# Attention query tiles: two whole ScalarE copies out of PSUM, and casts, low parts and sample parts made from the copy

## The chip, the cores and the metric

The kernel runs on one core of one Trainium2 chip. The metric is device time in microseconds (us). All times of the kernel before are from three runs and one profiled execution.

## The reference, cut to what matters

One layer of a hybrid decoder is computed for 512 prompt tokens, 16 meta tokens and 32 sample tokens (8 sequences of 4): a SwiGLU feed-forward block, then a gated linear attention branch and a stick-breaking attention branch side by side, a gated output projection, and a second SwiGLU block. The change lies in the stick-breaking branch, in the projection `q_b` and in what is made of it:

```python
q_b = q_b.reshape(B, L, SB_HEADS, SB_HEAD_DIM)      # 16 heads of 64
z = jnp.einsum('bqhd,bkhd->bhqk', qblk, k).astype(jnp.float32) * scale + bias_f   # scale = 64 ** -0.5 = 0.125
l = jnp.where(mask, jax.nn.log_sigmoid(-z), 0.0)
r = lax.cumsum(l, axis=3, reverse=True) - l
a = jnp.where(mask, jnp.exp(jax.nn.log_sigmoid(z) + r), 0.0)
return jnp.einsum('bhqk,bkhd->bqhd', a.astype(v.dtype), v)
```

## The kernel before

**Precision.** A product of two fp32 matrices is made of three TensorE products in the type fp32r: each operand is written as a high part (a cast, mostly on ScalarE) plus a low part (operand minus high part, on VectorE), and high x high, high x low and low x high are summed in PSUM. So each weight tile costs a ScalarE cast and a VectorE subtraction before TensorE can use it. In the profile these are the lines L1006 (cast, in `parted`) and L172 (the helper `tt`, called by `parted_lo`) for the weights of the key and value products, and L706 for those of the queries.

**Order.** The program is one loop of steps. A generator yields after about six matmuls (`tile_steps`: eight steps for a tile; `seven_steps`: fourteen); after each yield, `step()` runs the callbacks that `later(n, f)` placed n steps ahead, and then the callbacks that a table `at` holds for that step. ScalarE, VectorE, TensorE and GpSimd work in the order in which the program issues to them, so a callback's place in that order is its place in the queue of its engine.

**The attention stage.** The 16 heads go in 8 pairs. `BEGIN[pr]` is the step at which pair `pr` begins; from pair 1 on, a pair has 8 steps for `Pair.queries` and 14 for `Pair.values_keys`, which makes keys and values together by seven products of half size (a Strassen-like form) in four PSUM accumulators a, d, b, c. Its order is: a (2 steps), d (2), b (2), d again (2), c (2), a again (2), c again (2). Between them ScalarE copies a into b (L1069, 2 steps in; b goes on from there), d into a tile `e5` (L1059, 4 steps in; TensorE's second d product has to wait for that copy), b into c (L1069, 6 steps in) and b into a tile `u2` (L1059, 6 steps in). The third of the four weight tiles, `b2`, is the one that the second d product uses: its high part is cast 2 steps in (L1006) and its low part made 3 steps in (L172).

During the same steps the scores of the pair before are worked off: `scores` (two products, then two sigmoids on ScalarE, L2010 and L2011), `scan` (L2024, VectorE), `weigh` (L172 with 1343 columns, VectorE, and two small copies, L2035), `rows_k` (four transposes, L2041, and a ScalarE copy, L2043), `turned` (transposes of the weighed scores, L2086, and ScalarE copies, L2089), `summed` (L2102). For pairs 4 to 7 ScalarE also copies turned cache keys (L2191).

**Accumulator banks.** There are four, handed out in turn. The two that `queries` fills for its halves of 280 and 264 columns are the third and fourth that `values_keys` takes right behind it: the first half's bank becomes b, the second half's bank becomes c. So the copy of a into b can't start before everything that reads the first query half has read it.

**The queries now.** When the last product of `queries` is issued, the program issues at once: four ScalarE activations (L1925; 64 partitions x 280 or 232 columns: scale by 0.125, high part into `qs`), four small VectorE instructions (L1936; the sample tokens' queries into the tiles `qz`), and four VectorE instructions (L175; the low part, from PSUM and the high part). All twelve read the two PSUM banks.

**Memory.** All work tiles but a few live in one arena, and a table `PLACES`, one byte for each `take`, says at which slot each tile of the program lies. A tile that reuses a slot waits for the last reader of the tile before.

Of the kernel before, what the change touches and what calls it, by code (L numbers as in the profile page):

```python
# [19 lines left out]
NP = 512  # L20
NS = 32
NM = 16
NT = NP + NS + NM
HW = NT // 2
# [26 lines left out]


PLACES = bytes.fromhex("""
06241813202a5c3c5478117282764a7c688e328660846e8c92747a4c7034644e58567e38486a0c04948800401e804290666c8a4452304e500d44
2e5a3a6202360c100f16125c3e20223c2a1e401464344c0c48387e70568800046a94666c06504e464290304480288a262418081c62026e8e363a
327a86605a2e7c76922a5e078310848c694a885674520c504e0d689272082e1907062c1c8d5c2a8284855a1a6950740d83680f188c56082c850a
5e4e0b5a2a0684822e520c0d74696857585083075e0b562c5c5a820d8c0c2e69842a8306587557742c0a560d5e5c690c842e680d08828d83742c
8c565c060c07845e680d826975748c0856585957065c0d0c608468748c82908670667a446c948e0f4c808a0d266e7e30486a365458281a1c4024
3e52184e501e3c5a0f8a060d272b2d2a403e245a56262c0d408a3e3f2c0e8b3c243d0d3c8a2c400d413d3f3e3c5a361e30348b3c0a061a74821c
14948a0b3f7e62428c68902b28252429404e4a58546c5634888009723e263c0b0d8e18437c3063757f698395646a12702b16460850918d451d15  # L60
1b762d2a2f2e4d1000065384020f6e923304660d0a8a0e7a76518672484c503e3c32520f3031330d0e8f8e305070326a7c52085c645e0d602236
3880203a6216685a1e4e9042467e8f44741a941d2c824a121c2e262a8d648c28245c18658e0c5e0d1458360f4c2a6a3a16541a2e628015947c75
20448e2c82306450702652658d8c22386c48297432568f5e4458420c20365c0f1c1480942890300e7c467568182c094c82086465701e22297e60
5b5030565458325a2423908e4e12888c6c340c5e25186882493a4c0e16626a7c7d4446752e787438284208604011224a524870887e6c648c142a
2c5e12341c806a68829475627c16371e5b5249250e10701e36485d5e1a121888162514280c2a78493770885b1e27522c2e123718193628162578
3b141a70522a48125b0c1e2136254a4c880c11203b52141a7810121e185d708816252a521a5b364878100c133b122118162e142a1e2c20381052
3688701e5b2512211a0d362c4c4a2c25200c783b88702e212a52181614291e122c387888365b0d3a1a1e25123870480f3617200d0c1a78522c2a
182e2188113a141a0f4c4a12255b1678881e3614100c783b12141352705c2e2a18365e1a5b2c263828780e3a521e13885e25481a702c1a521416
1270884d7836383a2e5c2a4818124a78200c0e1e2636282c561e482a545b2e5e2594341c908e4c227438102c941a141652563a365d26784a1850
2c941c201e125174565b3490248e4c5b481e2226285d1a74501814123416514a564c52788e525074942c1c1856204a1a1e5c4c2250485e561c20  # L70
541e12342e4c2b2214165b1a182d2e5212502a1f5a344e32485856541c1e22305a2e122d34522c504e2a32481614585412202248181e1c1a582c
2e248e345474350e287826884e0c7090955250943637781012343214163b74905494702e78372a2c745c4a907556393b3655324c74944a377890
363b555a06303e646200600246726604806e40763c6a428c84686c513682927e867c588e28484f4a544c8a377d7a1e0c20223a440e181c4e8988
7b241a7c263a5051122a70106a167a5456888a483637902e421478647a828e92284d4b593e587437367e6c868c7a68844e774b3c403d6e6f417a
6651796571756b11364e94153f91430004506072620238462c4c0c9476204a181c0e241e487c681a8a445a08286684888e92828c7e6c86565a7a
323034122e1614422a103c5e6a6e0b4f40643a0809382374781f2426575854285990705c3d7a273f524e2307643940223a5a24547a362141285e
25501f372738225c09540a08642639407b3c2458076551287a20081e065326563b3c3938641f365452207a501e65245853082607063b3e3c5236
2051656424223a087a533b1f063e1e365150272664243a215320381e060a7a087e64024a72346c606862368a923a26200e82428c88128e761810
942c1c2a52864e505a2e40561a362c2454182a583c1f1c1d2c191b181c592a5657581d1856581c1d591b19181a3c425a36133a14221a5718121e
1517561c067e20688886  # L80
""")


class Arena:
# [13 lines left out]
    def take(self, width, dt=F32):  # L98
        k, s = -(-width // self.UNIT), next(self.places)
        c, n = self.column(s)  # L100
        assert all(self.free[s : s + k]) and s + k <= c + n, f"no room for {width} at {s}"
        if c not in self.tile or self.tile[c].dtype != dt:
            assert all(self.free[c : c + n]), f"two types at {c}"
            self.made += 1
            self.tile[c] = self.pool.tile([P, n * self.UNIT], dt, tag=f"room{c}", name=f"room{c}_{self.made}")
        self.free[s : s + k] = [False] * k
        a = self.tile[c][:, (s - c) * self.UNIT : (s - c) * self.UNIT + width]
        self.held[id(a)] = (a, s, k)
        return a
# [27 lines left out]
def hybrid_step(  # L137
# [26 lines left out]
    def ps(tag="ps"):  # L164
        count[0] += 1
        if tag == "acc":
            banks.append(banks.pop(0))
            return pa.tile([P, 512], F32, tag=f"acc{banks[-1]}", name=f"acc{count[0]}")
        return pp.tile([P, 512], F32, tag=tag, name=f"{tag}{count[0]}")

    def tt(out, a, b, op, eng=None):
        (eng or V).tensor_tensor(out=out, in0=a, in1=b, op=op)  # L172

    def stt(out, a, s, b, op0, op1):
        V.scalar_tensor_tensor(out=out, in0=a, scalar=s, in1=b, op0=op0, op1=op1)  # L175
# [91 lines left out]
    W2 = (HW, W1)  # L267
# [25 lines left out]
    for g in range(4):  # L293
        r_ = slice(NS * g, NS * g + NS)
# [470 lines left out]
    def later(n, f):  # L765
        todo.append([n, f])
# [154 lines left out]
    class Gain:  # L921
# [586 lines left out]
    for kind, what, n in MIXER:  # L1508
        w, c = {"r": (win, C_RA), "a": (win, C_GA), "b": (win, C_GB), "o": (w_o_gla[0], 0), "p": (w_o_sb[0], 0)}[what]
# [5 lines left out]
    with tc.manual_schedule(engines={E.PE, E.DVE, E.Activation, E.Pool}):  # L1515
# [72 lines left out]
        for j in range(2):  # L1588
            c = slice(P * j, P * j + P)
# [188 lines left out]
        for e in range(2):  # L1778
            acc = {h: ps("acc") for h in range(2)}
# [13 lines left out]
        p = ps()  # L1793
        for j in range(5):
            n = P if j < 4 else NTL
# [31 lines left out]
        for hd, head in enumerate(HEADS):  # L1827
# [54 lines left out]
    def qzp(pr, more=128):  # L1882
        return qz[pr // 2][:, 256 * (pr % 2) : 256 * (pr % 2) + 128 + more]

    own_, other = (slice(0, 64), slice(64, P)), (slice(64, P), slice(0, 64))
# [17 lines left out]
    class Pair:  # L1903
# [9 lines left out]
        def queries(self):  # L1913
            pr = self.pr
            acc = yield from tile_steps(um, W1)

            self.qs = qs = [take(NP, F32R) for _ in range(2)]
            def out(part):
                for h in range(2):
                    for e in range(2):  # L1920
                        c = slice(h * HW, min(NP, h * HW + HW))
                        src = acc[h][own_[e], : c.stop - c.start]
                        hi = qs[e][own_[e], c]
                        if part == 0:
                            S.activation(hi, src, AF.Copy, scale=0.125)  # L1925
                        else:
                            stt(qs[e][other[e], c], src, 0.125, hi.bitcast(F32), ALU.mult, ALU.subtract)

            out(0)
            for e in range(2):  # L1930
                r_ = slice(64 * e, 64 * e + 64)
                for g in range(2):

                    o = qzp(pr, 160)[r_, 128 * g : 128 * g + 160].rearrange("p (b x) -> p b x", x=40)[:, :, 4 * e : 4 * e + 4]
                    src = acc[1][r_, NP - HW + 16 * g : NP - HW + 16 * g + 16].rearrange("p (b t) -> p b t", t=4)
                    V.tensor_scalar(out=o, in0=src, scalar1=0.125, scalar2=None, op0=ALU.mult)  # L1936
            out(1)

        def keys(self):
            pr = self.pr  # L1940
# [554 lines left out]
    with tc.manual_schedule(engines={E.PE, E.DVE, E.Activation, E.Pool}):  # L2495
# [8 lines left out]
        starts, n = {}, -MIX0  # L2504
# [49 lines left out]
        for pr in range(8):  # L2554
            now, n, after = Pair(pr), BEGIN[pr + 1], BEGIN[pr + 2] if pr < 7 else BEGIN[8] + 20
# [25 lines left out]
        n, w0 = BEGIN[8], Weights(0)  # L2581
# [16 lines left out]
        n = 0  # L2598
# [29 lines left out]
        n = 8 * len(PAGES)  # L2628
# [43 lines left out]
        n = 0  # L2672
# [18 lines left out]
        for i, (n, h) in enumerate([(n, 0) for n in range(8)] + [(n, 1) for n in range(7, -1, -1)]):  # L2691
# [12 lines left out]
            acc = product(ms, (h,), held[n])  # L2704
# [94 lines left out]
```

## Time and profile before

| | |
|---|---|
| median of 3 runs | 1504.53 us (1504.02 to 1506.23) |
| profiled execution, own time | 1504.86 us |
| its span, first to last instruction | 1503.2 us |
| TensorE matmul busy | 1484.8 us |
| VectorE busy | 1099.9 us |
| ScalarE busy | 821.2 us |
| mean granted TensorE clock | 0.997 |

The own time of the profiled execution lies 1.7 us over its span and 0.3 us over the median. The span's first part is the first feed-forward block, then come the projections and the gated linear attention, then the attention stage with the eight pairs (about 566 to 800 us from the span's start, pairs 1 to 7 from about 583 us on), then the gates, the output projection and the second block.

### The profile page before, as it was taken

The page shows a single profiled execution, that of the slowest core. Times are in us where ns is not written, and L with a number is a line of the kernel's source. Part 1 is how long each engine was busy: PE and PEld are TensorE (multiplying, and loading weights), DVE is VectorE, ACT ScalarE, POOL GpSimd, SP SyncE. Part 2 cuts the span into 40 slices and gives each one's busy share as a digit, 9 for nine tenths or more (in the row PEclk, how much of TensorE's full clock was granted, in tenths as well). Part 3 has the DMA queues.
Part 4 walks back from the last instruction along what each step waited for, and adds up shares of the span by engine and source line. Part 5 has one row for each costly group of instructions (what it writes and reads, how often), then busy time and mean ns, then how long its engine had stood idle before and what let it go on. Part 6 is the DMA issues. An engine that isn't in the chain of part 4 may idle for free.

```text
span 1503.2 us, 29783 instructions
## 1 busy us (share of the span) xinstructions
PE 1484.8 (99%) x11825; PEld 1431.1 (95%) x11825; DVE 1099.9 (73%) x1860; ACT 821.2 (55%) x1537; POOL 78.0 (5%) x175
## 2 busy tenths in 40 slices
PE   9999999999999999999999999999999999999998
PEld 8999999999999889888889899999999999999998
DVE  5888888954677867877777844666567898888544
ACT  6455454533655657676776643644564555455334
POOL 2000000000000011211211000000000000000000
PEclk9999999999999999999999999999999999999999
DMA  8133333324665687457577767434532333333243
GB/s 250 51 91 99 99 99 93 93 78 139 168 142 132 160 160 154 110 107 134 137 112 177 224 166 206 100 99 136 163 108 69 90 108 99 99 99 89 88 146 121
DMA packets 288541, 187.61 MB, mean 125 GB/s; under 512 B 10988, under 2 KB 266674, under 8 KB 288402
## 3 DMA queue, kind: packets, MB, share of 16 engines
q1 hardware_dynamic: 280706, 181.97, 45.7%
q0 software_dynamic: 7680, 3.74, 2.3%
q8 instruction: 93, 1.52, 0.4%
q14 instruction: 46, 0.38, 0.1%
q10 hardware_dynamic: 16, 0.00, 0.0%
HBM read 160.63 MB, written 25.03 MB: 124 GB/s over the span
## 4 chain that ended last, share of the span: by engine, by line
PE 90%; DVE 5%; ACT 3%; issue 1%; DMA 0%; DVEq 0%; ACTq 0%; SPq 0%
PE acc L1301 8%; PE acc L1302 8%; PE acc L1300 8%; PE acc L741 6%; PE acc L744 6%; PE acc L742 6%; PE acc L728 5%; PE acc L729 4%; PE acc L731 4%; PE acc L1079 3%; PE acc L1081 3%; PE acc L1080 3%; PE acc L1239 2%; PE acc L1242 2%; PE acc L1240 2%; DVE room L172 2%
## 5 line engine op out<-in xcount | busy, mean ns | idle before, releaser
L172 DVE TENSOR_TENSOR room<-room,room 128x544 fp32r<-128x544 f32 (+18 forms) x443 | 286.1, 665 | 83.6 <-ACT room L1059 18.6
L172 DVE TENSOR_TENSOR lo<-raw,hi 128x1024 fp32r<-128x1024 f32 (+1 forms) x207 | 247.9, 1198 | 100.9 <-ACT hi L1006 59.9
L1301 PE MATMUL acc<-room,hi 128*128 128x280 f32 (+1 forms) x896 | 259.9, 290 | 0.0
L1302 PE MATMUL acc<-room,lo 128*128 128x280 f32 (+1 forms) x896 | 259.4, 289 | 0.0
L1300 PE MATMUL acc<-room,hi 128*128 128x280 f32 (+1 forms) x896 | 259.2, 289 | 0.0
L1006 ACT CAST hi<-raw 128x1024 fp32r<-128x1024 f32 x114 | 119.4, 1051 | 141.8 <-PE acc L1301 48.9
L728 PE MATMUL acc<-room,hi 128*128 128x280 f32 x608 | 175.7, 306 | 0.2 <-DVE room L175 0.2
L1302 PEld LDWEIGHTS acc<-room,lo 128*128 128x128 f32 x896 | 168.9, 188 | 0.0
L1301 PEld LDWEIGHTS acc<-room,hi 128*128 128x128 f32 x896 | 168.6, 188 | 0.0
L1300 PEld LDWEIGHTS acc<-room,hi 128*128 128x128 f32 x896 | 168.6, 188 | 0.0
L729 PE MATMUL acc<-room,hi 128*128 128x280 f32 x608 | 163.7, 289 | 0.0
L1079 PE MATMUL acc<-room,hi 128*128 128x280 f32 x476 | 147.6, 310 | 2.6 <-ACT room L1059 1.8
L1081 PE MATMUL acc<-room,lo 128*128 128x280 f32 (+1 forms) x476 | 139.9, 294 | 3.4 <-DVE lo L172 3.3
L1080 PE MATMUL acc<-room,hi 128*128 128x280 f32 (+1 forms) x476 | 139.2, 293 | 0.0
L706 ACT CAST hi<-raw 128x1024 fp32r<-128x1024 f32 (+1 forms) x93 | 93.5, 1006 | 77.9 <-issue 20.4
L1006 ACT CAST hi<-room 128x1024 fp32r<-128x1024 f32 x106 | 88.9, 838 | 82.2 <-PE acc L1301 60.0
L172 DVE TENSOR_TENSOR lo<-room,hi 128x1024 fp32r<-128x1024 f32 x106 | 101.1, 953 | 43.7 <-ACT hi L1006 43.3
L731 PE MATMUL acc<-room,lo 128*128 128x280 f32 x608 | 126.0, 288 | 0.0
L728 PEld LDWEIGHTS acc<-room,hi 128*128 128x128 f32 x608 | 114.5, 188 | 7.3 <-issue 5.6
L729 PEld LDWEIGHTS acc<-room,hi 128*128 128x128 f32 x608 | 114.7, 189 | 0.6
L741 PE MATMUL acc<-room,hi 128*128 128x280 f32 (+2 forms) x388 | 110.7, 295 | 0.0
L742 PE MATMUL acc<-room,hi 128*128 128x280 f32 (+2 forms) x388 | 108.7, 290 | 0.0
(405 smaller groups left out, 3614.4 us busy)
## 6 DMA issues: line engine op xcount, KB each, us to landing
raw<-in_w_in_dram SPq DMA_DIRECT2D x68, 256.0 KB, 5.1
raw<-in_ffn_w_gate_dram SPq DMA_DIRECT2D x64, 256.0 KB, 3.1
raw<-in_ffn_w_up_dram SPq DMA_DIRECT2D x64, 256.0 KB, 3.4
raw<-in_ffn_w_down_dram SPq DMA_DIRECT2D x36, 448.0 KB, 3.8
raw<-in_w_in_dram SPq DMA_DIRECT2D x29, 512.0 KB, 7.7
out_dram<-room SPq DMA_DIRECT2D x36, 256.0 KB, 4.8
room<-in_cache_k_dram SPq DMA_DIRECT2D x32, 256.0 KB, 5.4
room<-in_cache_v_dram SPq DMA_DIRECT2D x32, 256.0 KB, 6.1
```

What stands on the lines that cost most here:

```text
L172: (eng or V).tensor_tensor(out=out, in0=a, in1=b, op=op)
L728: T.matmul(acc[h][:, :w], hi[k], act.get(k, h, w)[0], start=(k == order[0]), stop=False, skip_group_check=True)
L729: T.matmul(acc[h][:, : wid[h]], hi[k], a[h][1], start=False, stop=False, skip_group_check=True)
L731: T.matmul(acc[h][:, : wid[h]], lo[k], a[h][0], start=False, stop=(k == order[-1]), skip_group_check=True)
L741: T.matmul(acc[h][:nw, : wid[h]], wh, a[h][0], start=(k == 0), stop=False)
L742: T.matmul(acc[h][:nw, : wid[h]], wh, a[h][1], start=False, stop=False)
L1006: S.copy(hi[:, :kt], src)
L1079: T.matmul(x[:, :n], hi, act_[k][0][:, :n], start=(first and k == 0), stop=False, skip_group_check=True)
L1081: T.matmul(x[:, :w], lo, act_[k][0][:, :w], start=False, stop=(k == 3), skip_group_check=True)
L1300: T.matmul(x[:, :QW], hi, act[k][0], start=(first and k == 0), stop=False, skip_group_check=True)
L1301: T.matmul(x[:, :QW], hi, act[k][1], start=False, stop=False, skip_group_check=True)
L1302: T.matmul(x[:, :QW], lo, act[k][0], start=False, stop=(k == 3), skip_group_check=True)
```

## The change

In `Pair.queries`, two ScalarE copies move the whole accumulators (128 partitions x 280 and x 264 columns), scaled by 0.125, into one fp32 tile `qf`. Nothing else reads the PSUM banks. From `qf` the rest is made some steps later: the sample parts (four small VectorE copies) 3 steps on, the high parts (two ScalarE casts of 64 partitions x 512 columns) 6 and 9 steps on, the low parts (two VectorE subtractions of that size) 8 and 11 steps on. The tiles `qs` are taken 6 steps later than before; `qf` is held for 11 steps. As the list of tiles is another one, the table `PLACES` is another one from its first byte to its last.

```diff
-            self.qs = qs = [take(NP, F32R) for _ in range(2)]
-            def out(part):
-                for h in range(2):
-                    for e in range(2):
-                        c = slice(h * HW, min(NP, h * HW + HW))
-                        src = acc[h][own_[e], : c.stop - c.start]
-                        hi = qs[e][own_[e], c]
-                        if part == 0:
-                            S.activation(hi, src, AF.Copy, scale=0.125)
-                        else:
-                            stt(qs[e][other[e], c], src, 0.125, hi.bitcast(F32), ALU.mult, ALU.subtract)
-
-            out(0)
-            for e in range(2):
-                r_ = slice(64 * e, 64 * e + 64)
-                for g in range(2):
-
-                    o = qzp(pr, 160)[r_, 128 * g : 128 * g + 160].rearrange("p (b x) -> p b x", x=40)[:, :, 4 * e : 4 * e + 4]
-                    src = acc[1][r_, NP - HW + 16 * g : NP - HW + 16 * g + 16].rearrange("p (b t) -> p b t", t=4)
-                    V.tensor_scalar(out=o, in0=src, scalar1=0.125, scalar2=None, op0=ALU.mult)
-            out(1)
+            qf = take(NT)
+            for h in range(2):
+                S.activation(qf[:, h * HW : h * HW + W2[h]], acc[h][:, : W2[h]], AF.Copy, scale=0.125)
+
+            def samples():
+                for e in range(2):
+                    r_ = slice(64 * e, 64 * e + 64)
+                    for g in range(2):
+
+                        o = qzp(pr, 160)[r_, 128 * g : 128 * g + 160].rearrange("p (b x) -> p b x", x=40)[:, :, 4 * e : 4 * e + 4]
+                        V.tensor_copy(o, qf[r_, NP + 16 * g : NP + 16 * g + 16].rearrange("p (b t) -> p b t", t=4))
+
+            def hi(e):
+                if e == 0:
+                    self.qs = [take(NP, F32R) for _ in range(2)]
+                S.copy(self.qs[e][own_[e]], qf[own_[e], :NP])
+
+            def lo(e):
+                tt(self.qs[e][other[e]], qf[own_[e], :NP], self.qs[e][own_[e]].bitcast(F32), ALU.subtract)
+                if e:
+                    give(qf)
+
+            for n, f in ((3, samples), (6, lambda: hi(0)), (8, lambda: lo(0)), (9, lambda: hi(1)), (11, lambda: lo(1))):
+                later(n, f)
```

`PLACES` is left out here: 27 lines of hexadecimal digits stand in the place of 27 others.

More of the change, by code (lines that the diff above doesn't have):

```diff
@@ L53 @@
 PLACES = bytes.fromhex("""
[L54 to L77, printed above, removed]
@@ L78 @@
-2051656424223a087a533b1f063e1e365150272664243a215320381e060a7a087e64024a72346c606862368a923a26200e82428c88128e761810
-942c1c2a52864e505a2e40561a362c2454182a583c1f1c1d2c191b181c592a5657581d1856581c1d591b19181a3c425a36133a14221a5718121e
-1517561c067e20688886
+0c4236301f4f2a3d163453647c0256726c6088544a94901c187648867866922414128c8e748a5c00847e684106706e7a80620408244c581a5b07
+2e826a28265c4e231e0a062a5e5a3e3c30401e082292784e8c66748e1284207e6886008a0c43104c62047a6e1a585c708036253a826a601c1802
+549456640c6c4a9033422c852a5272302e76484e2615882f1046297c840c246c892b13363a42723b282a3038324e102e472f6c1452242b88892a
@@ new lines @@
+3a122d4e283332720e0c304246526d73242e114e88103b72322c3a422852316c262a254e46241110723230423a526c6d880e31254e2924517210
+504442526d893a305144286c4f88722489504e3b51263a5428426c464488728e8c941e867a80744f68606457517866008a705a6e921c3a361a18
+55381614123c0c641a1c2a324e3057182451550c641931241c1b565251311a552419271a55192752511c1a1d1b0c5a2a3e64001a3c1b01030400
+0205552750201e384636221970788a72644e5084488e0824260a3d88606c7e3052666a3a824b45473779421f86928c901b7a3e43123923738b21
+7180191d181a30577c7407683c32761233941606146e55624031807e584c30886052564a0732336d6c5552666a068c8256923e3286907a5a3010
@@ new lines @@
+6c2e0c54720a5e86365c2a2c0e78181a3a32462851444f201904420070718a1e221c388b299110024e54724c490a323a1a462e567a824800664b
+9290296a185185420c061e847071588e443005288c6c040854028a725e2c0e2a1c4c103e4e0082931858390c866691516a90707142843849784a
+92185a205c22004854362826026c8a8c58042e7237448208390c0a387a568691246a66253a901e1a78648a8e5593421c49584a348c6c82707204
+32304c085e8452864e507a91923e562a0d061e37420a581a2f5530240c088c4c4a49100e5642323458372a04450749060c1e420e47442a2c551a
+1c588c06560c044c242e4207371e1a49553230443435100e068c3a4238371c3004550c2432492b1e1a55078c1c2c0637100e4230463804443a34
@@ new lines @@
+2a4332071e090c248c55491c1a34062b303242492a0b8c0e244d303a04441e1a1c384637422c8c58100c3255062e304649372a422c3034350810
+0e0b2a8c061e1a1c380444372e3a2c56240c0849432a0a3a55308c2e0437428c0624351e381a1c462c442a04434b308c49080a322e550d1e2a49
+37303442042e1e30340e1009448c2c1a1c324638068c0a553a240c344b49205c571a2c463a4d3443378438087a902a495e26285c8430044b2e32
+5456451a0a068c4284381e5e20364d082c5c321c587a905c2a20491a18422e8c4530324b080a4d36062c04907a04308c84385e04061e2e2c5c2a
+20494237341e063008494b2c32465e5c42394d0a20364432044b3b494a2c00023708221e065c5a303244483600043b4a4c372c4302390a06485a
@@ new lines @@
+5e44205c1e2242000a1c263b06048d541a3656185884907a8c484c0f0e06104a243a0c8c283837392c0e04900a08020007367a062a34103b3a2f
+0c46080a2a2c37062e7b2f0c4e307c827a62923994663e706e8668403c728a166a7678457e1480125c742a5a1a5e6c1c182660427f89841e4c64
+75582220568e7489886c2e542c747f45483b0a02248a8926496036427e1982048c72067c892a1a181c7e805e085b5a1589785c768e886a80147e
+3f5f86896987683c9412258b7d3a09734616900788830b006212287a92704266906484741e3e7e2280385654264c6c6a36201a2a184a6010944e
+0c78028e521a312e500e0a048c061612143a5a7624085e44682b35832c542a728656883d34421c8a437c481830763283405d772c3d543f69575b
@@ L81 @@
+8a432a685a7688554230821b5f69342e8b3e198a3d3c761c182a4654595a68578b4288835f8a3c32182a3e1954821a348b444059696876305f2a
+888a83823c188b421a5a6859463e5f2a76548a69403c8842828b5989461a5f545a2a402c6876888a6a828e028010060c8c922a94907866707404
+427e6c120a7a22524e3a1e40285e5a5c54202e2a1c30783666221e1a3c7018192c2a22207823181f1e21792a2e1e201f78232179222a54123e20
+34322242471e78703c335a64443082922062
 """)
```

## The prediction

> **What bounds the kernel now.** I read the page first: TensorE's matmuls are busy for 99% of the span, so a change elsewhere pays only where TensorE waits or runs slowly.
>
> ```profile
> PE 1484.8 (99%) x11825; PEld 1431.1 (95%) x11825; DVE 1099.9 (73%) x1860; ACT 821.2 (55%) x1537; POOL 78.0 (5%) x175
> ```
>
> Second, the waits of TensorE in the stretch of pairs 1 to 7 (583 to 800 us).
>
> ```profile
> core 0 of [0], span 1503.2 us
> engine line waited for: us in total, times, longest us
> PE acc L1081 <- DVE lo L172: 3.3, 3, 1.1
> PE ps L2086 <- DVE room L172: 2.3, 3, 0.8
> PE acc L1079 <- ACT room L1059: 1.8, 3, 1.0
> PE ps L2189 <- ACT room L2043: 1.2, 1, 1.2
> PE acc L1079 <- ACT acc L1069: 0.5, 1, 0.5
> PE ps L2203 <- ACT room L2191: 0.3, 1, 0.3
> ```
>
> These sum to 9.4 us: half of the 18.4 us that TensorE is idle at all (1503.2 - 1484.8) lies here, in 217 us of 1503. Third, the same stretch's clock, by windows (length, then busy us and count for PE, PEld, DVE, ACT, POOL, granted PE clock, DMA share, GB/s).
>
> ```profile
> 601.26:604.67 3.41, 1.93 (x14) 1.69 (x14) 3.34 (x8) 2.77 (x8) 1.78 (x2) 1.00 0.15 32
> 628.56:631.97 3.41, 2.76 (x21) 2.17 (x19) 3.32 (x7) 2.65 (x5) 0.76 (x2) 1.00 0.00 0
> 631.98:635.38 3.40, 3.33 (x14) 2.98 (x14) 3.33 (x7) 2.83 (x7) 1.57 (x2) 0.50 0.28 60
> 662.70:666.10 3.40, 1.66 (x11) 1.43 (x12) 3.33 (x6) 2.88 (x7) 1.55 (x2) 1.00 0.24 70
> 666.11:669.51 3.40, 3.40 (x17) 3.38 (x17) 3.23 (x6) 1.06 (x2) 1.54 (x2) 0.50 0.77 214
> ```
> ```profile
> 630.96 1.03 PE L2170 MATMUL ps<-ones,room 1*128 1x1 f32 x8
> ```
>
> Twice, in pairs 2 and 3, the clock is halved for 3.4 us, right behind a stretch in which TensorE had little to do: 1.66 us of work in 3.40, and 2.76 of which 1.0 is eight products of one element (the last row, from the timeline). A stretch with 1.93 was not followed by it. Half speed for 3.4 us loses 1.7 us of work; two cost 3.4. So 9.4 + 3.4 = 12.8 us is the most that a cure of this stage can give.
>
> Fourth, why TensorE waits there: the timeline of pair 3, ScalarE (two fences), then VectorE, then TensorE (start, us, engine, line; in brackets the idle time before and its releaser).
>
> ```profile
> 656.95 1.54 ACT L1925 ACTIVATE room<-acc 64x280 fp32r<-64x280 f32 x4
> 660.06 0.38 ACT L1069 COPY acc<-acc 128x280 f32<-128x280 f32 x1 [1.57 <-DVE room L175]
> ```
> ```profile
> 662.88 0.41 ACT L1059 COPY room<-acc 128x280 f32<-128x280 f32 x1
> ```
> ```profile
> 656.33 1.25 DVE L2024 TENSOR_TENSOR_SCAN room<-room,room 128x528 f32<-128x528 f32 x1
> 658.52 0.53 DVE L1936 TENSOR_SCALAR room<-acc 64x16 f32<-64x16 f32 x4 [0.94 <-ACT room L1925]
> 659.07 1.75 DVE L175 SCALAR_TENSOR_TENSOR room<-acc,room 64x280 fp32r<-64x280 f32 x4
> 660.85 1.07 DVE L2024 TENSOR_TENSOR_SCAN room<-room,room 128x144 f32<-128x144 f32 x2
> 661.84 1.58 DVE L172 TENSOR_TENSOR room<-room,room 128x1343 f32<-128x1343 f32 x1
> 663.45 0.33 DVE L2035 COPY room<-room 128x96 f32<-128x96 f32 x2
> 663.70 1.22 DVE L172 TENSOR_TENSOR lo<-raw,hi 128x1024 fp32r<-128x1024 f32 x1
> ```
> ```profile
> 662.02 0.29 PE L1081 MATMUL acc<-room,lo 128*128 128x280 f32 x1
> 663.34 0.40 PE L1079 MATMUL acc<-room,hi 128*128 128x280 f32 x1 [1.03 <-ACT room L1059]
> 663.58 0.29 PE L1080 MATMUL acc<-room,hi 128*128 128x280 f32 x1
> 664.97 0.40 PE L1081 MATMUL acc<-room,lo 128*128 128x280 f32 x1 [1.10 <-DVE lo L172]
> ```
>
> The reader is to see a double hold. VectorE stands at L1936 until ScalarE has made the high parts. Then ScalarE stands at the copy of a into b, 1.57 us, until VectorE has made the first half's low parts, for b is the first query half's bank. Behind that copy in ScalarE's queue stand two sigmoids, the cast of `b2`, the row copy and the `e5` copy (662.88); behind the twelve query instructions in VectorE's queue stand scans, the weighing (661.84) and the low part of `b2` (663.70). TensorE waits for `e5` first, for `b2`'s low part next. That it is so in nearly every pair show the waits of ScalarE and of VectorE in the same stretch:
>
> ```profile
> ACT room L2089 <- PE ps L2086: 18.2, 21, 1.4
> ACT acc L1069 <- DVE room L175: 9.5, 6, 1.6
> ```
> ```profile
> DVE lo L172 <- ACT hi L1006: 22.4, 7, 3.6
> DVE room L1936 <- ACT room L1925: 7.1, 6, 2.0
> ```
>
> **The change part by part.** The removed instructions' durations stand above: four activations take 1.54 us (L1925 x4), four low parts 1.75 (L175 x4). For the added ones the nearest groups of pairs 1 to 7 (last: busy us, mean ns, idle before):
>
> ```profile
> L1958 ACT CAST room<-room 64x528 fp32r<-64x528 f32 x14 | 8.8, 632 | 0.3
> ...
> L1976 ACT COPY room<-acc 128x280 f32<-128x280 f32 x7 | 2.8, 393 | 0.0
> ```
> ```profile
> L172 DVE TENSOR_TENSOR room<-room,room 64x528 fp32r<-64x528 f32 x13 | 9.1, 703 | 0.5
> ```
>
> *ScalarE, total.* Removed 1.54 us a pair; added two copies at 0.39 and two casts near 0.62 (the row has 528 columns, the cast 512), 2.02. It gains 0.5 us of work a pair, 4 us over eight pairs. It lies beside TensorE: ScalarE waits 18.2 us in seven pairs for turned scores alone (L2089), 2.6 a pair.
>
> *VectorE, total.* Removed 1.75; added two subtractions at 0.70, 1.40. The four sample copies stay at 0.53 together, with the read of PSUM gone; bounds 0.2 either way, I take no change. VectorE loses 0.35 us of work a pair.
>
> *Order at the critical place, pair 3.* ScalarE finishes two copies at 656.95 + 0.75 = 657.7 and copies a into b at once (done about 658.1, 2.3 us sooner). The queue behind it moves up by as much: from the start of that copy to the end of `e5` is 663.29 - 660.06 = 3.23 us, so `e5` would be there at 660.9. TensorE asks for it at 662.3, when the last product before the wait has gone. That wait goes, margin 1.4. The wait for b itself (0.5) goes with the earlier copy.
>
> VectorE is free at 657.58 and goes straight to the next scans. Of the time until it starts `b2`'s low part, 663.70 - 657.58 = 6.12 us, the wait of 0.94 and the low parts of 1.75 go; the samples, 3 steps on, still stand ahead of it. Start 661.0, end 662.2. TensorE wants it one matmul pair (0.25 us) behind 662.3. That wait goes, with only 0.3 us to spare: the samples are what eats the margin. Bounds: the three waits of this kind gone (3.3), or, if it comes 0.5 us late in each, 1.8 gone.
>
> *The casts put off.* `hi(0)` comes 6 steps on, ahead of the copy b into c, which the second accumulator c needs 2 steps later. It puts 0.6 us in front of a queue that has become 2 us earlier; nobody waits. `lo(0)` and `lo(1)` (8 and 11 steps on) stand ahead of the pieces that end keys and values. Cover: between pairs VectorE stands idle until a cast of the next weights (L172 for L1006 above, 22.4 us), 3.2 us a pair against 1.4 us moved there. `qs` is wanted about 13 steps after `hi(0)`. If that cover went, up to 1.4 us a pair would fall on TensorE.
>
> *What is late next.* The transposes of the weighed scores (L2086) wait for the second weighing (the second row of TensorE's waits). VectorE reaches it 2.7 us sooner (663.70 - 661.0); TensorE, rid of its own waits, also comes sooner, in pair 3 by 2.1 us and 1.7 for the clock. Their 2.3 us I leave as they are; bounds: all gone (-2.3), or 0.7 more in each of pairs 2 and 3, where the halved clock hid them (+1.4).
>
> *The row copy.* One wait of 1.2 us (L2189 for L2043) stems from ScalarE held by VectorE:
>
> ```profile
> 755.43 0.59 ACT L2043 COPY room<-ps 128x512 f32<-128x512 f32 x1 [0.99 <-DVE room L172]
> ```
>
> The copy's slot was still read by the weighing, which now comes 2.7 us sooner: gone.
>
> *The new places.* No row of before shows them. Nearest row: the wait above, a reused slot, 0.99 us, of which TensorE paid 1.2. One such wait more or fewer in each of two pairs is +-2.4. Outside pairs 1 to 7 TensorE's idle time is 18.4 - 9.4 = 9 us in 1286, so little can be gained there. I take 0. The issue of DMAs isn't moved; a shorter pair asks the DMA engines for more per us, but they are busy for 0.47 of pair 3 (row under rival 2).
>
> *Sum.* Gone: 3.3 (low part of `b2`) + 1.8 (`e5`) + 1.2 (row copy) + 0.5 (b) = 6.8. The halved clock: both stretches follow a shortage that holds such waits (2.1 us of them in pair 3; 0.5 in pair 2, whose shortage would shrink to 2.76 + 0.5 of work), so both go, 3.4. Together 10.2. The profiled execution took 1504.86 us (span 1503.2 and 1.7 around it), 0.3 over the median 1504.53; taken off the median this is **1494.3 us**.
>
> [...]
>
> **The rivals.**
> 1. *The halved stretches stay.* They hang on something other than the waits. For it: in pair 1 a window with 1.93 us of work had no such sequel, while one with 2.76 had. Against: the 1.0 us of one-element products explains that one. Time 1504.5 - 6.8 = 1497.7. [...]
> 2. *VectorE becomes the bound.* Only what ScalarE caused goes (1.8 + 0.5 + 1.2 = 3.5), and `b2`'s low part stays late because margins of 0.3 us don't hold. For it: VectorE is busy for 24.4 us of 31 in pair 3 (below). Against: the 3.2 us of idle time between pairs. Time 1501.0.
>
> ```profile
> 645.00:676.00 31.00, 28.87 (x206) 26.40 (x204) 24.37 (x45) 21.26 (x41) 5.77 (x10) 0.94 0.47 104
> ```
>
> 3. *The gain is eaten.* The change does what it says, but new waits for slots or for `hi(0)` take back 8 to 12 us, 1 to 2 a pair. For it: the table is wholly new, and the cast of 0.6 us now stands ahead of two accumulator copies. Against: ScalarE has 1.4 us of margin there. Time about 1504.
> 4. *Slower.* One mechanism: `qf`'s slot is read until late, so the first copy of each pair stands behind VectorE, as L2043 did, and both banks stay held. The price before was 1.57 us at that copy; it turns the sign when the hold is over 3 us in each of seven pairs, as it must spend the 2.7 us that VectorE is ahead and then cost TensorE 0.5 us more a pair: 1504.5 + 3.5 = 1508. Against: slots given back last before `qf` is taken were read by VectorE's work before the scan that starts at 656.33, ahead of 656.95.
>
> **How the numbers follow.** Forecast 0.62, rival 1 0.10, rival 2 0.10, rival 3 0.10, rival 4 0.08. About 0.2% (3 us) is what a measurement of this kernel can tell from no change. Faster: forecast, rival 1, and most of rival 2, whose 3.5 us sits near the bound: 0.79. Same: rest of rival 2, and rival 3: 0.13. Slower: 0.08. The forecast's own range is 1490.7 (two slot waits fewer, 1.2 of the transposes' waits gone) to 1498.1 (two more, transposes 1.4 worse). The range that holds 8 in 10 reaches from there over rivals 1 and 2: 1490.5 to 1502.5.
>
> **What would show it.** After: no wait of L1069 for the queries' VectorE work; copies of queries ending 0.8 us after the start; L1081 and L1079 off the list of TensorE's waits; the granted clock at 1.00 in all windows of pairs 2 and 3; pair 3 shorter by 3 to 4 us; L2086 still waiting for L172, 1 to 4 us in all. The forecast is wrong if L1081 still waits for `lo`, if a halved stretch is left, or if the copies to `qf` stand behind VectorE.

## The result, and the profile after

| | before | after |
|---|---|---|
| median (range), 4 runs each on one chip | 1505.38 us (1504.02 to 1506.76) | 1493.01 us (1492.25 to 1494.5) |
| ratio to before, 95% interval | | 0.9919 [0.9902, 0.9936] |
| profiled execution: span | 1503.2 us | 1490.7 us |

The forecast was 1494.3 us. In a second comparison the changed kernel took 1493.05 us (1492.72 to 1494.44, five runs; 0.9921 [0.9907, 0.9934]). One of the ten runs of experiment 5 took 1777.24 us at a mean granted clock of 0.753; the figures given there are those of the other nine.

In the new file the lines behind the change stand three further down: L2086 is now L2089, L2189 is L2192, L1059 to L1081 keep their numbers. First the busy times of the page, then the waits of TensorE and of its weight loads in pairs 1 to 7:

```profile
PE 1477.2 (99%) x11825; PEld 1426.3 (96%) x11825; DVE 1099.8 (74%) x1844; ACT 822.7 (55%) x1537; POOL 86.6 (6%) x175
```
```profile
PE ps L2089 <- DVE room L172: 2.3, 4, 0.8
PE ps L2171 <- POOL room L2159: 0.9, 1, 0.9
PE ps L2206 <- ACT room L2194: 0.6, 2, 0.3
```

L1081, L1079 and L2192 are off the list. One wait is new: L2171, the transpose of a table of sample rows that GpSimd makes once, in pair 2. TensorE's idle time fell from 18.4 to 1490.7 - 1477.2 = 13.5 us, 4.9 less; its busy time fell by 7.6 with the same instructions. The half clock accounts for up to 3.4 of that; the rest suggests that part of a stall is booked as busy time of a neighbouring instruction. The waits of the weight loads (PEld) give fuller figures. Before, in the same stretch:

```profile
PEld acc L1081 <- DVE lo L172: 4.4, 4, 1.3
PEld acc L1079 <- ACT room L1059: 2.5, 3, 1.3
...
PEld ps L2189 <- ACT room L2043: 2.2, 3, 1.4
PEld ps L2086 <- DVE room L172: 2.0, 2, 1.0
...
PEld acc L1079 <- ACT acc L1069: 1.0, 2, 0.8
...
PEld ps L2086 <- ACT room L1059: 0.9, 1, 0.9
```

And after:

```profile
PEld ps L2089 <- DVE room L172: 2.8, 3, 1.0
...
PEld ps L2171 <- POOL room L2159: 1.1, 1, 1.1
...
PEld ps L2089 <- PE acc L1081: 0.4, 1, 0.4
```

The four waits that went are 4.4 + 2.5 + 2.2 + 1.0 = 10.1 here, against 6.8 in the list of the matmuls. With the 3.4 of the clock and 1.1 taken off for L2171 that is 12.4 us, and the span is shorter by 12.5. That the two meet so closely is luck: smaller rows left out here moved too (waits for sigmoids at L2061 and L2189, 1.7, went; 0.8 came at L2206 and L2089), and the 3.4 is too high, as the point on the half clock below shows.

Pair 3, ScalarE, VectorE and TensorE:

```profile
651.50 0.71 ACT L1919 ACTIVATE room<-acc 128x280 f32<-128x280 f32 x2
652.70 0.38 ACT L1069 COPY acc<-acc 128x280 f32<-128x280 f32 x1 [0.49 <-PE acc L1081]
```
```profile
655.54 0.41 ACT L1059 COPY room<-acc 128x280 f32<-128x280 f32 x1
```
```profile
655.84 0.50 DVE L1927 COPY room<-room 64x16 f32<-64x16 f32 x4
656.37 1.23 DVE L172 TENSOR_TENSOR lo<-raw,hi 128x1024 fp32r<-128x1024 f32 x1
```
```profile
657.65 0.40 PE L1081 MATMUL acc<-room,lo 128*128 128x280 f32 x1
```

The banks are free 0.71 us after the copies begin. The copy of a into b waits now for TensorE's own product of a, no longer for VectorE. VectorE has no wait for the queries; `b2`'s low part ends at 657.60, and TensorE uses it at 657.65. The list shows no stall there, and there is no margin either.

### The profile page after: what moved, and what is told of

The parts are those of the page before. It is cut to its first block, busy times and chain, and to the rows that moved or that the text cites. A ratio compares the mean times of both kernels' runs of the same rounds, so it can differ in the third digit from the quotient of the medians.

```text
span 1490.7 us, 29755 instructions
## 1 busy us (share of the span) xinstructions
PE 1477.2 (99%) x11825; PEld 1426.3 (96%) x11825; DVE 1099.8 (74%) x1844; ACT 822.7 (55%) x1537; POOL 86.6 (6%) x175
## 4 chain that ended last, share of the span: by engine, by line
PE 53%; DVE 3%; ACT 1%; DMA 1%; issue 0%; DVEq 0%; SPq 0%; ACTq 0%
PE acc L1300 4%; PE acc L1301 4%; PE acc L1302 4%; PE acc L1079 3%; PE acc L744 3%; PE acc L742 3%; PE acc L741 3%; PE acc L1080 3%; PE acc L1081 3%; PE acc L728 3%; PE acc L731 3%; PE acc L729 3%; PE ps L2105 1%; DVE room L172 1%; PE ps L2089 1%; PE acc L1239 1%
## 5 line engine op out<-in xcount | busy, mean ns | idle before, releaser
L172 DVE TENSOR_TENSOR room<-room,room 128x560 f32<-128x560 f32 (+15 forms) x469 | 303.3, 666 | 82.1 <-ACT room L808 17.8
L1079 PE MATMUL acc<-room,hi 128*128 128x280 f32 x476 | 146.2, 307 | 0.4 <-ACT acc L1069 0.2
L1081 PE MATMUL acc<-room,lo 128*128 128x280 f32 (+1 forms) x476 | 138.3, 290 | 0.0
```

The source lines that it names most:

```text
L1079: T.matmul(x[:, :n], hi, act_[k][0][:, :n], start=(first and k == 0), stop=False, skip_group_check=True)
L1081: T.matmul(x[:, :w], lo, act_[k][0][:, :w], start=False, stop=(k == 3), skip_group_check=True)
```

## The experiments

All times are medians; each ratio is to the kernel before on the same chip.

**1. The order or the table: the changed code with the old table.** The places of the 24 tiles that are new are put into it, and 6 others are moved for them (begin of the first line of each):

```diff
 PLACES = bytes.fromhex("""
-0c4236301f4f2a3d163453647c0256726c608854
...
+06241813202a5c3c5478117282764a7c688e3286
...
```

> The changed code with the placement table of the kernel before: the tiles of which both kernels have the same keep the place in SBUF that they had before, 6 others are moved to make room for the 24 tiles that are new or live at other times. Theory (the order of the work makes the gain, and where a tile lies costs nothing): 1493, within 1.5 us of the changed kernel. Rival (the new table took away or brought waits between tiles that share a place, and makes the gain): 1503 to 1505. If it lies between, the difference to 1493 is the table's part.

Measured: 1497.39 us, ratio 0.9946 [0.9930, 0.9963]. It lies between: by this the order of the work gives some 8 us and the table some 4. The loss lies in pair 2: from its first product of L2105 to the next pair's it takes 34.02 us, with the new table 29.03. TensorE's waits of the copies, of `b2`'s low part and of the row copy are gone here too. New in its size is one row:

```profile
PE ps L2171 <- POOL room L2159: 3.1, 1, 3.1
```

ScalarE, then GpSimd, in pair 2 (GpSimd's L2018 selects mask the tiles that ScalarE's L2014 has written):

```profile
624.68 0.61 ACT L2013 ACTIVATE room<-ps,sbb 128x416 f32<-128x416 f32 x1 [1.32 <-DVE lo L172]
```
```profile
625.85 3.12 POOL L2018 TENSOR_SCALAR_AFFINE_SELECT room<-room 128x128 f32<-128x128 f32 x2 [3.23 <-ACT room L2014]
```

The sigmoid's tile lies where a weight tile lay, which its low part still reads. The same wait stood in the kernel before:

```profile
ACT room L2010 <- DVE lo L172: 1.3, 1, 1.3
```

**2. The same with GpSimd's chain begun earlier.** The callback that is moved also makes two small VectorE copies (L2164, 0.6 to 0.7 us together), and two entries of the table change places, as its tiles are taken sooner.

```diff
-        then(BEGIN[2] + 8, sample_rows)
+        then(BEGIN[2] + 4, sample_rows)
```

> The kernel with the changed code and the old placement table, with GpSimd's chain for the sample rows (L2153 to L2159) begun at BEGIN[2] + 4 and not + 8. In the trace of the old table ScalarE's exponential of pair 2 (L2013) waits 1.3 us for a place that a low part of a weight still reads, GpSimd's mask select behind it is late by as much and slow, and TensorE waits 3.1 us for GpSimd at L2171, followed by 6.8 us of half clock. Theory (the old table costs its 4.4 us nearly all through that one chain): TensorE's wait at L2171 and the half clock go, 1493 to 1494 with at most 1 us of it for the front. Rival (the table costs in many small places, and L2171 only shows their sum): 1496 to 1497.

Measured: 1492.8 us, 0.9917 [0.9902, 0.9932]. L2171 is off TensorE's list and pair 2 takes 29.20 us, while the slot wait is still there and even longer:

```profile
ACT room L2013 <- DVE lo L172: 1.8, 1, 1.8
```

So the old table costs most of its 4.4 us through the one chain from that slot over ScalarE and GpSimd to L2171, with the half clock behind it (6.8 us in the trace with the old table); the slot wait alone costs little when nobody waits for GpSimd. Some 1 us may lie elsewhere, for the same move may save the new table's 0.9 at L2171 too; the changed kernel with this move alone was not run, and the share of the two VectorE copies is not known.

**3. VectorE made late, PSUM and ScalarE left free.** In the changed kernel, behind the two copies:

```diff
+            for _ in range(n):                    # n = 2, 3, 4
+                tt(wgk2, wgk2, wgk2, ALU.max)     # 16 x 512
```

> The changed kernel with two idle VectorE operations (16x512) where the query tile leaves PSUM, half of what brought back the whole loss. Theory (VectorE had no room there, each microsecond counts from the first on): at b2's low part (L1081) TensorE waits 1.0 to 1.3 us in each of four pairs, less the waits at L2089 that go (2.3 in all), with one or two half-clock stretches of 1.7: 1497 to 1500. Rival (a threshold: the loss comes only of the half clock that a stall of over 2 us brings): 1493 to 1495.

> The changed kernel with three idle VectorE operations (16x512) where the query tile leaves PSUM, between the two (1497.8, no half clock) and the four (1506.2, half clock in five windows of 3.4 us). Theory (each operation more costs its 0.7 us at b2's low part in four pairs, and from a stall of 1.7 us inside one window of 3.4 on, the next window has half clock): waits of 1.8 to 2.1 us at L1081, half clock behind those that lie in one window, two to four of them, 1.7 us each: 1502 to 1505. Rival (VectorE's time alone counts, and the clock adds nothing): 1500.5.

> The changed kernel with four idle VectorE operations (16x512, about 0.7 us each, 2.8 us in all, on a table that nobody reads any more) where the query tile leaves PSUM, in all eight tiles: VectorE is as late there as it was before, while PSUM and ScalarE are free. Theory M (VectorE's lateness alone sets the loss of pairs 1 to 4): 2 to 2.7 us come back in each of four pairs, 1501 to 1504. Theory S (the sum of single waits): the wait of b2's low part, 3.3 us, and the half-clock stretches that it brings, 1.7 to 3.4, so 1496.5 to 1500. Rival (VectorE has room for it, the gain came of PSUM and ScalarE): 1493 to 1494.

Measured: 1497.75 us (0.9949 [0.9933, 0.9964]), 1501.66 (0.9979 [0.9970, 0.9989]) and 1506.19 (1.0005 [0.9995, 1.0014]) for two, three and four. One added operation (from four), and TensorE's wait with two, three and four:

```profile
L172 DVE TENSOR_TENSOR wgk<-wgk 16x512 f32<-16x512 f32 x32 | 21.8, 680 | 0.8
```
```profile
PE acc L1081 <- DVE lo L172: 3.7, 3, 1.4
```
```profile
PE acc L1081 <- DVE lo L172: 6.3, 3, 2.1
```
```profile
PE acc L1081 <- DVE lo L172: 10.0, 4, 2.7
```

Four operations are 2.72 us a tile, about what the prediction gave as VectorE's lead (0.94 + 1.75 = 2.69), and they bring back the whole gain with PSUM free. The wait grows from the first microsecond, as an end at 657.60 for a use at 657.65 lets expect: 1.36 us added, up to 1.4 waited. With four, the transposes of the weighed scores are off the list, since TensorE comes later than they do. The time with four, 2.2 us above theory M's upper end, is made of the waits and the clock: its trace has 17 us at half clock in five windows. That would be 8.5 us of lost work, but it costs less: the one of the ten runs with a mean granted clock of 0.999 took 1503.31 us, the nine with 0.993 to 0.995 took 1505.47 to 1507.45. With two operations there is no half clock (mean granted clock 0.999). With three there are three such windows (0.996), and the time lies 0.3 below the theory's range and 1.2 above the rival's: the waits came as expected, the clock cost less than the 1.7 a window that the theory took. With two and three, part of the loss is a longer wait for GpSimd's table (1.4 and 1.6 us, in the changed kernel 0.9).

**4. ScalarE held, VectorE left free.**

```diff
+            for _ in range(4):
+                S.copy(wgk2, wgk2)                # 16 x 512
```

> The changed kernel with four idle ScalarE copies (16x512, about 0.6 us each, 2.3 us in all) behind the two copies out of PSUM, in all eight tiles: ScalarE is held as long as it was before, while VectorE has its gain. Theory M (the longer of the two holds sets the loss, and 2.3 us on ScalarE is nearly as long as VectorE's 2.7): 1.5 to 2.3 us back in pairs 1 to 4, 1499 to 1502. Theory S (single waits): the evictions' waits 1.8 and 0.5 and the cast of b2 later by the hold, 0 to 1.5: 1495.5 to 1497. Rival (ScalarE's hold was covered): 1493 to 1494.

Measured: 1495.02 us, 0.9933 [0.9916, 0.9950]. One added copy, and the weight loads' waits for the copy to `e5`:

```profile
L1921 ACT COPY wgk<-wgk 16x512 f32<-16x512 f32 x32 | 19.7, 615 | 0.8
```
```profile
PEld acc L1079 <- ACT room L1059: 1.1, 3, 0.4
```

2.46 us a tile, more than the 1.57 that ScalarE stood before, cost 2.0 us in all, of which the trace puts 1.1 to these waits and 0.6 to `b2`'s low part, whose cast comes later; there is also one stretch of half clock (mean granted clock 0.999), at the place where the second profile of the changed kernel has one. The time lies 0.5 below theory S's range and 1 above the rival's; theory M, by which ScalarE's hold is worth nearly as much as VectorE's, falls. The margin of 1.4 us for `e5` in the prediction covers part of it.

**5. In the kernel before, only the samples issued last.**

```diff
             out(0)
+            out(1)
             for e in range(2):
...
-            out(1)
```

> The kernel before with one edit: the four sample copies of the queries (L1936) are issued after the second low part and not between the first low part and the second cast. ScalarE's second cast then no longer stands behind VectorE, so its 1.57 us hold per tile goes, and VectorE's wait of 0.94 us for that cast gets shorter; the two low parts out of PSUM stay where they are. Theory M (the two holds run side by side and the longer, VectorE's chain of low parts and its waits, sets the loss): some 0.9 to 1.1 us back in each of pairs 1 to 4, 1.2 for the row copy, so 1499 to 1501. Theory S (the prediction's sum: each vanished wait counts by itself): the waits on the two evictions, 1.8 and 0.5, the row copy, 1.2, and half of the 3.3 of b2's low part: 5.2 us, and one of the half-clock stretches, so 1498.5 to 1500, with the evictions' waits gone from TensorE's list and the low part's still there. Rival (only the low parts' 1.75 us on VectorE count): 1504 to 1505.

In the kernel before, the program issues the four high parts, then the samples, then the four low parts; the edit puts the low parts first. What the expectation calls ScalarE's second cast is, by its 1.57 us, the copy of a into b.

Measured: 1501.39 us (1500.22 to 1503.12), 0.9977 [0.9968, 0.9987], 0.4 us above theory M's range and 1.4 above theory S's. In pair 3 the hold of that copy fell from 1.57 to 0.28 us and VectorE's wait for the high parts from 0.94 to 0.20. TensorE's waits say why little came of it. The waits for `e5` and b are off TensorE's list, as in S, but `b2`'s low part did not get better by a half; its wait nearly doubled:

```profile
PE acc L1081 <- DVE lo L172: 6.1, 4, 1.7
```

In the kernel before, TensorE waited for `e5` (1.8) and then for the low part (3.3). Both came of one delay: what it had waited for the first, it need not wait for the second. Taking the first away mostly moves the wait. The trace has three stretches of half clock, one more than before (mean granted clock 0.995 against 0.997), and the time is still 3.8 us shorter.

**6. The samples made later, in the changed kernel.**

```diff
-            ((3, samples), (6, lambda: hi(0)), (8, lambda: lo(0)), (9, lambda: hi(1)), (11, lambda: lo(1)))
+            ((6, lambda: hi(0)), (8, lambda: lo(0)), (9, lambda: hi(1)), (11, samples), (11, lambda: lo(1)))
```

> The changed kernel with one number changed: the four sample copies of the queries (L1927, 0.50 us on VectorE in a tile) are made at step 11, just ahead of the second low part, and not at step 3, ahead of b2's low part and of the second weighing. Theory (VectorE's chain up to the second weighing still ends last in pairs 1 to 4, where TensorE waits 2.3 us in four places, L2089): each of these waits gets shorter by up to 0.5, with the part of a stall that the gaps do not show, some 1.7 us in all: 1491 to 1491.5. Rival (another wait is late next, or 0.5 us of VectorE is covered): 1493.

Measured: 1494.09 us (1493.84 to 1494.89), 0.9927 [0.9913, 0.9940]: no gain. Half of the theory came true; the other half went to GpSimd:

```profile
PE ps L2171 <- POOL room L2159: 2.4, 1, 2.4
...
PE ps L2089 <- DVE room L172: 0.6, 2, 0.3
```

The wait at L2089 fell from 2.3 to 0.6, and pairs 3 and 4 are 0.6 us shorter each. But L2171 waits 2.4 and not 0.9, and a stretch of half clock follows (mean granted clock 0.999). GpSimd in pair 2 and VectorE at the same time, changed kernel first, then this one:

```profile
624.50 2.77 POOL L2157 TENSOR_SCALAR_AFFINE_SELECT room<-room 32x64 f32<-32x64 f32 x1
627.34 0.39 POOL L2159 TENSOR_SCALAR_AFFINE_SELECT room<-room 32x64 f32<-32x64 f32 x1
627.70 0.39 POOL L2157 TENSOR_SCALAR_AFFINE_SELECT room<-room 32x64 f32<-32x64 f32 x1
```
```profile
625.48 1.52 DVE L172 TENSOR_TENSOR room<-room,room 128x1343 f32<-128x1343 f32 x1
627.03 0.35 DVE L2038 COPY room<-room 128x96 f32<-128x96 f32 x2
627.31 0.83 DVE L1927 COPY room<-room 64x16 f32<-64x16 f32 x4
```
```profile
625.29 2.77 POOL L2157 TENSOR_SCALAR_AFFINE_SELECT room<-room 32x64 f32<-32x64 f32 x1
628.13 1.43 POOL L2159 TENSOR_SCALAR_AFFINE_SELECT room<-room 32x64 f32<-32x64 f32 x1
629.53 0.91 POOL L2157 TENSOR_SCALAR_AFFINE_SELECT room<-room 32x64 f32<-32x64 f32 x1
```
```profile
627.83 0.35 DVE L2038 COPY room<-room 128x96 f32<-128x96 f32 x2
628.10 1.21 DVE L172 TENSOR_TENSOR lo<-raw,hi 128x1024 fp32r<-128x1024 f32 x1
```

In these rows a select took 0.39 us beside VectorE's copies, and 0.91 to 2.77 beside its scans, weighing and low parts. The changed kernel's fourth select, at 628.16, took 0.39 too; it began just ahead of the low part at 628.17, which took 1.40 us for its usual 1.2. The sample copies had been the opening through which GpSimd ended its chain; the edit closed it.

**7. Late samples, and GpSimd's chain earlier** (as in 2, at `BEGIN[2] + 4`, then at `BEGIN[2]`; here too a few entries of the table change places).

> The kernel of the late samples (L1927 at step 11), with the rows that GpSimd makes for the samples (the chain of L2153 to L2159, one time in pair 2) begun at BEGIN[2] + 4 and not + 8, when VectorE is not in its run of scans and weighing. Theory: the 0.9 us that TensorE waits for that chain at L2171 goes, with 0.2 of a stall that its gap does not show: 1 us below the late samples alone, 1490 to 1490.5. Rival (the selects are slow there too, or the transposes of the weighed scores wait in its place): the same as the late samples alone.

> As the version with late samples and rows begun at BEGIN[2] + 4, with the rows begun at BEGIN[2]: in the version of + 4 one select of the chain still took 4.7 us, the five mask selects behind it ended late, and TensorE waited 1.1 us at L2089 in pair 2, against 0.3 in pairs 3 and 4. Theory (GpSimd is slow only beside VectorE's back-to-back work of two inputs, and had 12 us with nothing to do ahead of that stretch): the 1.1 us wait falls to 0.3, pair 2 gets shorter by 0.8 to 1, 1489 to 1489.8. Rival (VectorE's low parts run there too, the selects are as slow, and nothing changes): 1490.3.

Measured: 1490.3 us (0.9902 [0.9887, 0.9917]) and 1489.08 us (1487.93 to 1490.15; 0.9893 [0.9878, 0.9908]). The second ran beside the changed kernel's 1493.05, and the two ranges of runs don't meet, though the intervals of the ratios just touch: it beats both kernels. Both times lie in the range of their theory, the first partly by luck: the late samples alone had come out at 1494.09 and not at 1491, and the move took off 3.8 us and not 1, of which L2171's wait was 2.4. GpSimd's third select with the chain at + 4, and the first two selects with the chain at the pair's begin:

```profile
619.60 4.72 POOL L2157 TENSOR_SCALAR_AFFINE_SELECT room<-room 32x64 f32<-32x64 f32 x1
```
```profile
606.28 0.65 POOL L2157 TENSOR_SCALAR_AFFINE_SELECT room<-room 32x64 f32<-32x64 f32 x1
607.00 0.39 POOL L2159 TENSOR_SCALAR_AFFINE_SELECT room<-room 32x64 f32<-32x64 f32 x1
```

TensorE's waits at the transposes fell from 1.7 to 0.6 us, and L2171 is off the list.

## Why the prediction was right, point by point

- **The double hold** was the cause, and it goes. What the sum took as separate additions was one chain. VectorE's end of it carries it: 2.7 us given back to VectorE undo the change (experiment 3), 2.5 given to ScalarE cost a sixth of it (4). The 1.8 of `e5` was a symptom: cured alone, it came back at L1081 (5). The sum of both was still right, because both ends went together.
- **Two terms were mis-sized**, in opposite directions. "6.8 gone" is too low: the rows of the matmuls under-read a stall; by the weight loads' rows the same four waits were 10.1. The 3.4 of the half clock is too high (below). The gain was 12.4 us against 10.2 forecast, from a median before of 1505.38 and not 1504.53; that the time came within 1.3 us is partly luck.
- **The margin** of 0.3 us for `b2`'s low part was rightly called thin, and was thinner: 0.05. That three waits did not turn into partial ones, as the lower bound had it, hung on this. `e5`'s margin of 1.4 us held.
- **The transposes** were left at 2.3 us: they stood at 2.3, and at 2.1 in the second profile.
- **The new places** were taken as 0, with bounds of 2.4. This step failed in size: with the old table the change is 4.4 us worse (1). Yet not by what I bounded, a slot wait of ScalarE that TensorE pays at the next copy, but by one that ScalarE hands on to GpSimd.
- **GpSimd** has no term in the prediction. Its chain was ready in time before and, by the times of its selects, for a reason that the change removes: in pair 2 its four selects ran while VectorE stood for the queries' high parts and then read PSUM, and took 0.39 to 0.40 us each, 1.7 in all. In the changed kernel the first ran beside scans and the weighing (2.77 us, experiment 6), and the four took 4.05 in all. TensorE, which also came sooner, had to wait 0.9 us (1.1 by the weight loads). It is the price that the sum lacked. The kernel before, GpSimd's first select and VectorE:

```profile
627.28 0.40 POOL L2154 TENSOR_SCALAR_AFFINE_SELECT room<-room 32x64 f32<-32x64 f32 x1
```
```profile
627.76 0.53 DVE L1936 TENSOR_SCALAR room<-acc 64x16 f32<-64x16 f32 x4 [1.12 <-ACT room L1925]
```

- **The half clock.** Both stretches were gone in the profile after. In the second profile of the same kernel one was there, at 629.5 us, so by that profile one of the prediction's own signs of being wrong, a halved stretch that is left, was met. Pair 2 took 29.03 us without it and 30.25 with it: it cost 1.2 us, not 1.7. Of the 43 runs of the kernel before that stand beside the experiments, the seven with a mean granted clock of 0.999 (at most about one stretch) took 1503.52 to 1504.94, the two with 0.994 took 1506.51 and 1506.68. The changed kernel's five runs at 0.999 took 1492.25 to 1493.52. At equal clock the gain is thus 11.6 us on the mean, and the clock's part of the 12.4 is nearer 1 us than 3.4, an estimate from these runs. A likely reason, not tested, is that at full speed TensorE would have waited for other engines instead. By this, some 1.5 us of the gain stand in no row of the weight loads' list. Rival 1 (the stretches stay, 1497.7) did not occur.
- **Pair 3** was to be 3 to 4 us shorter; from one pair's first product of L2102 to the next pair's it went from 30.92 us (645.13 to 676.05) to 27.61, in the row below at full clock. Pairs 2 to 7 got shorter by 2.3, 3.3, 1.9, 0.2, 1.8 and 0.8 us, what lies ahead of them by 2.3, and what lies behind them not at all.
- **Rivals 2 to 4.** VectorE is close to being the bound, as rival 2 said; the dose of experiment 3 shows where it would have begun. Of rival 3 one piece came, L2171. Rival 4 did not come: ScalarE's largest wait at this place, 9.5 us for the queries' work on VectorE before, is one for TensorE now (second row):

```profile
640.56:668.17 27.61, 26.85 (x206) 24.84 (x205) 23.90 (x43) 21.28 (x41) 7.52 (x10) 1.00 0.51 116
```
```profile
ACT acc L1069 <- PE acc L1081: 7.1, 8, 1.6
```

## What to carry to other kernels

Two engines that wait for each other behind one PSUM tile make one chain, so price its last end once, and test it by putting the lateness back on one engine at a time. When a stall goes, what had been in time only because of it comes next, and here that was an engine 6% busy; move such one-time work to where its engine has time to spare well ahead of the use. For the price of a wait take the weight loads' rows beside the matmuls', for here a stall also hid in busy time (10.1 us by the first, 6.8 by the second).

## What the runs showed of the hardware

**GpSimd beside VectorE.** One and the same select of 32x64 took 0.40 us with VectorE idle (the kernel before, 627.28), 0.39 beside VectorE's copies, and 0.91 to 2.77 beside its scans, weighing and low parts (experiment 6); of the 4.72 in experiment 7 VectorE's rows are not shown. The mask selects of L2018 (128x128) in the changed kernel go the same way: 0.29 us at 712.12, with VectorE idle from 711.55 to 713.02, and 1.41 at 654.30, beside the weighing (654.03 to 655.56). Not every one was slow there: at 618.84 one took 0.34, beside a low part (617.80 to 619.02). The runs show the times; they don't show the cause, nor that the number of inputs is what counts, as the theory of experiment 7 has it.

**Ahead of the half clock.** Windows of 3.41 us, the length of a halved stretch (length, PE, PEld, DVE, ACT, POOL busy, granted clock, DMA share, GB/s), first the kernel with three added operations: a stretch with little work, and the one after it.

```profile
660.79:664.20 3.41, 1.29 (x10) 1.06 (x10) 3.33 (x9) 1.70 (x5) 3.12 (x3) 1.00 0.27 56
664.21:667.61 3.40, 3.40 (x17) 3.39 (x16) 3.20 (x7) 0.74 (x2) 0.00 (x0) 0.50 1.04 156
```

The changed kernel in its first and second profile, around the same stall:

```profile
625.24:628.64 3.40, 2.52 (x20) 2.11 (x19) 3.32 (x9) 3.40 (x7) 3.26 (x5) 1.00 0.26 77
628.65:632.05 3.40, 3.40 (x28) 3.38 (x29) 3.27 (x10) 1.22 (x4) 3.40 (x4) 1.00 0.23 47
```
```profile
626.13:629.53 3.40, 2.52 (x21) 2.28 (x20) 3.32 (x9) 2.40 (x5) 3.26 (x6) 1.00 0.27 77
629.55:632.95 3.40, 3.40 (x17) 3.40 (x16) 3.18 (x10) 0.82 (x3) 3.10 (x3) 0.50 0.66 143
```
```profile
628.69 1.03 PE L2173 MATMUL ps<-ones,room 1*128 1x1 f32 x8
```
```profile
628.14 1.03 PE L2173 MATMUL ps<-ones,room 1*128 1x1 f32 x8
```

The stall of 0.88 us and the 1.03 us of one-element products fall into two windows in the first (the products begin at 628.69, behind the border at 628.65), and into one in the second, where the clock halves. Halved stretches of one profile lay whole lengths apart: in the kernel before they began at 631.98 and 666.11, ten times 3.413 us apart, and with three added operations at 633.49, 664.21 and 694.93, 30.72 or nine times 3.413 apart. The border at 628.65 is counted back, by 252 lengths, from the halved stretch at the end of the first profile (granted clock 0.50 from 1488.82 us on); in the second profile the halved stretch began at 629.55, so the two grids don't lie alike.

TensorE's idle time (the gaps, plus one-element products), in all windows of such a grid over pairs 1 to 7 at full clock, in the kernel before and in the first profile of the changed one: the two that half clock followed had 1.65 and 1.74 us; no other had more than 1.48. In the rows above, 2.12 us (three added operations) and 0.88 + 1.03 = 1.91 (second profile) were followed by half clock, and so was 2.96 with the old table, at 629.65 us. One window goes against a limit between 1.48 and 1.65: with three added operations, 1.95 us at 599.43 was not followed. Of the 1.65, 1.00 are one-element products; by its gaps alone, 0.65 us, that window would stand far below the one with 1.48, which was not followed. What sets off the half clock is not shown beyond these windows.
